# Making the down-projection's fp16 operands in the up-projection and keeping them in DRAM

## The chip, the core and the metric

The kernel runs on one core of a Trainium2 chip. The metric is the device time of one execution in microseconds; the median of several runs counts.

## What is computed

One layer of a hybrid block: four kinds of mixers on a sequence of 2048 tokens of width 1024, an output projection, and then a feed-forward part, which is where the change lies:

```python
u = rms_norm(h, norm_ffn_pre[layer])
f = jnp.square(jax.nn.relu(jnp.einsum('bsd,df->bsf', u, w_ff_up[layer])))
h = h + rms_norm(jnp.einsum('bsf,fd->bsd', f, w_ff_down[layer]), norm_ffn_post[layer])
```

Inputs and output are fp32; w_ff_up is 1024 x 4096, w_ff_down 4096 x 1024.

## The kernel before

**Products.** Every fp32 operand is split into an fp16 high and an fp16 low part (`split_to`: ACT copies to the high part, DVE subtracts for the low part), and a product is three fp16 matmuls (`mm3`). On top of that both projections multiply 2 x 2 blocks of blocks with seven products instead of eight. For that, four sums or differences of the four sub-blocks are formed first on POOL (`sums`, `diffs`), the seven operands are split in the order of `TURN`, and the results are added up behind the products. A block of the up- or down-projection is therefore seven products, numbered 0, 5, 1, 6, 4, 3, 2 in this order, into four PSUM accumulators: X (0, then 1), Y (5), Z (6, then 3) and V (4, then 2). Behind product 0 ACT copies X to s; DVE adds Y to s; behind 6 and 4 DVE makes c = s + Z and c += V; behind 3 and 2 it makes s + Z and s + V. An accumulator is written again only when it has been read.

**Up-projection** (`up_block`, called by `run`). The 4096 columns of f are 16 pairs g of 2 x 128; the tokens are two halves cp of 1024. A block (g, cp) is 84 matmuls of 128x512. `up_weights` prepares the weights of a pair up to two pairs ahead: two loads ur, two gain products (ur) and four sums (us) on POOL, a reduce for each load on DVE (a_up) and a maximum over them (m_up), which a small product p_up on PE spreads over the partitions, and seven splits (uw). `down_top` reads the rows of w_ff_down (dr) for their maximum (a_dn). Behind the products ACT applies relu and square into the tiles e, which `put` stores to DRAM (fD) as fp32, two stores a block.

**Down-projection** (`down_block`). The 16 pairs are taken in the six passes of `PASSES`: two of two pairs, four of three. A pass goes through eight blocks (cp, j) of 128 + 128 tokens, adding into the tiles y, which stay in SBUF. `down_weights` prepares the weights of a pass (dr, four differences ds on POOL, seven splits dw). For each block `f_operands` loads the fp32 f (fr), forms four sums on POOL (ft) and splits seven operands (fo) of 128 x n x 128, n being the pairs of the pass. In passes 1 to 5 POOL adds s to three of the four y parts. In the last pass `finish` normalizes: the sum of squares on ACT (fsq), ms_f, the product with the gain and rs_f on POOL, the last scaling on DVE, and the store.

**Order.** The program is recorded as operations in lanes, and `weave` writes them out by a list schedule: at each step it takes the operation with the earliest start by its own cost table, plus a tenth of a microsecond for each step of the lane's priority number. The engines then run their queues in that order, and SP issues all transfers from one queue. The up-blocks have priority number 2, the weights 1, the down-blocks 0. Nearly all instructions are recorded in one helper line, so the views name L557 for all of them.

Of the kernel before, what the change touches and what calls it, by code (L numbers as in the profile page):

```python
# [10 lines left out]
F32 = mybir.dt.float32  # L11
F16 = mybir.dt.float16
# [7 lines left out]
P = 128  # L20
# [11 lines left out]
U = 1024.0  # L32
UF = 256.0
TURN = (0, 5, 1, 6, 4, 3, 2)
PASSES = ((0, 2), (2, 4), (4, 7), (7, 10), (10, 13), (13, 16))
EPS = 1e-6
LAM_INIT = 0.8 - 0.6 * math.exp(-0.3 * 0)
# [58 lines left out]
class Halves:  # L96


    def __init__(self, tiles):
        self.tiles = tiles  # L100
        self.n = tiles[0].shape[1]
# [1477 lines left out]
def split_to(nc, src, hi, lo, scale=None):  # L1579
    if scale is None:  # L1580
        nc.scalar.activation(hi, src, AF.Copy)
        nc.vector.tensor_tensor(lo, src, hi, op=ALU.subtract)
    else:
        nc.scalar.activation(hi, src, AF.Copy, scale=scale)
        nc.vector.scalar_tensor_tensor(lo, src, scale, hi, op0=ALU.mult, op1=ALU.subtract)
# [29 lines left out]
class Ffn:  # L1615
# [8 lines left out]
    def __init__(self, k, w_up, w_dn, post, gain, u, ev, out):  # L1624
        self.k, self.w_dn, self.post, self.gain, self.u, self.ev, self.out = k, w_dn, post, gain, u, ev, out
        self.up = w_up.rearrange("(k p) f -> p k f", p=P)
        self.pairs = DFF // (2 * P)
        self.k0 = k.keep.tile([P, self.pairs], F32, tag="k0", name="k0")
        self.kd = k.keep.tile([P, self.pairs], F32, tag="kd", name="kd")
        self.f = [[k.dram.tile([4, P, 2 * (p1 - p0), 2 * P], F32, tag=f"fD{q}{cp}", name=f"fD{q}{cp}")  # L1630
                   for cp in range(2)] for q, (p0, p1) in enumerate(PASSES)]
        self.w, self.d, self.n = {}, {}, 0

    def banks(self, wide):
        self.n += 1
# [63 lines left out]
    def up_block(self, g, cp):  # L1699

        k, nc = self.k, self.k.nc
        u, w = self.u[cp], self.w[g]

        def prod(ps, i, fresh):
            for kt in range(4):
                with nc.fuse():
                    mm3(nc, ps, w[i][:, 0, kt, :], w[i][:, 1, kt, :], u[i][0][:, kt, :], u[i][1][:, kt, :], kt == 0,
                        kt == 3, fresh)

        def add(b):  # L1710
            c = self.ev.tile([P, 512], F32, tag="q", name=f"c{g}{cp}")
            nc.vector.tensor_tensor(c[:], s[:], b, op=ALU.add)
            return c

        def act(src, f, ab):
            d = e[f][:, :, ab, :]
            nc.scalar.activation(d, src.rearrange("p (j t) -> p j t", j=4), AF.Relu, scale=2.0 ** -24)
            nc.scalar.activation(d, d, AF.Square)

        def put(f):  # L1720
            x = 2 * (g - PASSES[q][0]) + f
            nc.sync.dma_start(self.f[q][cp][:, :, x, :].rearrange("j p c -> p j c"),
                              e[f][:].rearrange("p j a t -> p j (a t)"))
        q = next(i for i, (p0, p1) in enumerate(PASSES) if p0 <= g < p1)
        with nc.lane("up", 2):
            X, Y, Z, V = self.banks(False)
            nc.need(*u[TURN[-1]])
            s = k.fuw.tile([P, 512], F32, tag="s", name=f"us{g}{cp}", bufs=1)
            e = [k.fuw.tile([P, 4, 2, P], F32, tag="er", name=f"e{g}{cp}{f}", bufs=2) for f in range(2)]
            prod(X, 0, True)  # L1730
            nc.scalar.activation(s[:], X, AF.Copy)
            prod(Y, 5, True)
            nc.vector.tensor_tensor(s[:], s[:], Y, op=ALU.add)
            prod(X, 1, False)
            act(X, 0, 0)
            prod(Z, 6, True)
            c = add(Z)
            prod(V, 4, True)
            nc.vector.tensor_tensor(c[:], c[:], V, op=ALU.add)
            act(c[:], 1, 1)  # L1740
            prod(Z, 3, False)
            act(add(Z)[:], 1, 0)
            put(1)
            prod(V, 2, False)
            act(add(V)[:], 0, 1)
            put(0)

# [12 lines left out]
                split_to(nc, src, w[:, 0], w[:, 1], self.kd[:, g:g + 1])  # L1762

    def f_operands(self, q, cp, j):
        k, nc = self.k, self.k.nc
        n = PASSES[q][1] - PASSES[q][0]
        with nc.lane("fprep", 1):
            fr = k.fdr.tile([P, n, 2, 2, P], F32, tag="fr", name=f"fr{q}{cp}{j}", bufs=2)
            nc.sync.dma_start(fr[:].rearrange("p n f a t -> p (n f a t)"),
                              self.f[q][cp][j].rearrange("p f c -> p (f c)"))  # L1770
            x = fr[:, :, 0, 0, :], fr[:, :, 1, 0, :], fr[:, :, 0, 1, :], fr[:, :, 1, 1, :]
            z = [k.fue.tile([P, n, P], F32, tag="ct", name=f"ft{q}{cp}{j}", bufs=4)[:] for _ in range(4)]
            sums(nc.gpsimd, *x, *z)
            ops = {}
            for i, src in in_turn(*x, *z, False):
                w = ops[i] = k.fdr.tile([P, 2, n, P], F16, tag="fo", name=f"fo{q}{cp}{j}{i}", bufs=10)
                split_to(nc, src, w[:, 0], w[:, 1])
        return ops

    def down_block(self, q, cp, j):  # L1780

        k, nc = self.k, self.k.nc
        p0, p1 = PASSES[q]
        ops = self.f_operands(q, cp, j)
        ta, tb = cp * 8 + j, cp * 8 + 4 + j
        y, last = self.y, len(PASSES) - 1
        y11, y12, y21, y22 = y[ta][:, 0:512], y[ta][:, 512:], y[tb][:, 0:512], y[tb][:, 512:]

        def prod(ps, i, fresh):
            for x in range(p1 - p0):  # L1790
                w = self.d[p0 + x][i]
                with nc.fuse():
                    mm3(nc, ps, ops[i][:, 0, x, :], ops[i][:, 1, x, :], w[:, 0], w[:, 1], x == 0, x == p1 - p0 - 1, fresh)

        def add(o, a, b):
            nc.vector.tensor_tensor(o, a, b, op=ALU.add)
        with nc.lane("down", 0):
            if q == 0 and cp + j:
                nc.claim(y[ta], y[tb])
            X, Y, Z, V = self.banks(True)  # L1800
            s = k.fue.tile([P, 512], F32, tag="s", name=f"ds{q}{cp}{j}", bufs=2)[:]
            prod(X, 0, True)
            nc.scalar.activation(s, X, AF.Copy)
            prod(Y, 5, True)
            add(s, s, Y)
            if q:
                for o in (y22, y21, y12):
                    (nc.gpsimd if q < last or o is not y12 else nc.vector).tensor_tensor(o, o, s, op=ALU.add)
            prod(X, 1, False)
            if q:  # L1810
                add(y11, y11, X)
            else:
                nc.scalar.activation(y11, X, AF.Copy)
            prod(Z, 6, True)
            add(y22, y22 if q else s, Z)
            prod(V, 4, True)
            add(y22, y22, V)
            prod(Z, 3, False)
            add(y21, y21 if q else s, Z)
            prod(V, 2, False)  # L1820
            add(y12, y12 if q else s, V)
        if q == last:
            lo, hi, full = slice(0, 512), slice(512, D), slice(0, D)
            if (cp, j) == (1, 3):
                self.finish([(ta, lo), (tb, hi), (tb, lo), (ta, hi)])
            else:
                self.finish([(tb, full)])
                self.finish([(ta, full)])
# [32 lines left out]
    def run(self):  # L1861
        k, nc = self.k, self.k.nc
        n = self.pairs
        blocks = [(0, 0), (1, 0), (0, 1), (1, 1)] + [(g, cp) for g in range(2, n - 1) for cp in range(2)]
        blocks += [(n - 1, 1), (n - 1, 0)]
        ready = 0
        for g, cp in blocks:
            while ready < min(n, g + 2):
                self.up_weights(ready, 1)
                self.down_top(ready)  # L1870
                ready += 1
            self.up_block(g, cp)
        self.down_scale()
        self.y = [k.fd.tile([P, D], F32, tag=f"y{t}", name=f"y{t}") for t in range(NT)]
        for q, (p0, p1) in enumerate(PASSES):
            for g in range(p0, p1):
                self.down_weights(g, 2 if q else 0)
            if q == len(PASSES) - 1:
                with nc.lane("prep"):
                    self.gp = k.wpool.tile([P, D], F32, tag="wraw", name="fgp", bufs=2)  # L1880
                    nc.sync.dma_start(self.gp[:], self.post.to_broadcast([P, D]))
            for cp in range(2):
                for j in range(4):
                    self.down_block(q, cp, j)
# [133 lines left out]
```

## Time and profile before

| | us |
|---|---|
| three runs | 2641.31, 2648.63, 2649.54 |
| median | 2648.63 |
| the profiled execution, its own time | 2646.39 |
| its span | 2644.6 |

| engine | busy, us | share of the span |
|---|---|---|
| PE | 2457.6 | 93% |
| DVE | 1851.6 | 70% |
| ACT | 1294.7 | 49% |
| POOL | 1239.7 | 47% |

Shares are averages over the whole kernel; the mixers end at about 1300 us, the up-projection runs to about 1980, the down-projection to the end. Times in a view are microseconds from the start of the span. A view of groups gives, for each kind of instruction, the engine, the operation, output<-inputs by the program's tile names (numbers left out), the shapes, the count, and behind the bar the busy time in us and the mean of one in ns, then the engine's idle time ahead of them with what ended it. Matmul records overlap, so their pitch is read from the starts.

### The profile page before, as it was taken

The page shows a single profiled execution, that of the slowest core. Times are in us where ns is not written, and L with a number is a line of the kernel's source. Part 1 is how long each engine was busy: PE and PEld are TensorE (multiplying, and loading weights), DVE is VectorE, ACT ScalarE, POOL GpSimd, SP SyncE. Part 2 cuts the span into 40 slices and gives each one's busy share as a digit, 9 for nine tenths or more (in the row PEclk, how much of TensorE's full clock was granted, in tenths as well). Part 3 has the DMA queues.
Part 4 walks back from the last instruction along what each step waited for, and adds up shares of the span by engine and source line. Part 5 has one row for each costly group of instructions (what it writes and reads, how often), then busy time and mean ns, then how long its engine had stood idle before and what let it go on. Part 6 is the DMA issues. An engine that isn't in the chain of part 4 may idle for free.

```text
span 2644.6 us, 39843 instructions
## 1 busy us (share of the span) xinstructions
PE 2457.6 (93%) x14186; PEld 1298.7 (49%) x14186; DVE 1851.6 (70%) x3900; ACT 1294.7 (49%) x2647; POOL 1239.7 (47%) x1195
## 2 busy tenths in 40 slices
PE   7999999999999997988897999999998889898987
PEld 5555575656645565654444444444443334343433
DVE  6487986666798778766534555444459997979787
ACT  6377775434456676644444444444445443433332
POOL 5373331020265445447444222222235787878798
PEclk9999999999999998998997999999999999999999
DMA  6522225362351525235342433333333222222145
GB/s 185 152 70 85 83 74 186 71 183 45 82 152 53 149 83 162 83 113 159 112 128 88 128 113 126 119 99 117 120 108 123 76 89 68 88 67 90 64 143 155
DMA packets 276982, 290.30 MB, mean 110 GB/s; under 512 B 50420, under 2 KB 234676, under 8 KB 276271
## 3 DMA queue, kind: packets, MB, share of 16 engines
q1 hardware_dynamic: 276783, 287.75, 35.8%
q8 instruction: 112, 1.84, 0.3%
q14 instruction: 87, 0.71, 0.1%
HBM read 203.47 MB, written 91.04 MB: 111 GB/s over the span
## 4 chain that ended last, share of the span: by engine, by line
PE 31%; POOL 12%; DVE 8%; issue 7%; DMA 2%; ACT 1%; POOLq 0%; DVEq 0%; SPq 0%; ACTq 0%
PE mz L557 7%; PE mx L557 6%; PE mv L557 6%; POOL ft L557 5%; POOL y L557 4%; PE po L557 4%; PE my L557 3%; DVE fo L557 2%; DVE dw L557 2%; DVE y L557 1%; PE fut L557 1%; POOL rs_f L557 1%; DMA dr<-in_w_ff_down_dram 1%; POOL nt L557 1%; POOL ds L557 1%
## 5 line engine op out<-in xcount | busy, mean ns | idle before, releaser
L557 PEld LDWEIGHTS <-fo 128*128 128x128 f16 x2688 | 265.7, 99 | 399.3 <-issue 92.2
L557 PEld LDWEIGHTS <-uw 128*128 128x128 f16 x2688 | 264.1, 98 | 314.7 <-issue 5.6
L557 PE MATMUL pt<-uuh,wh 128*128 128x512 f16 x640 | 244.3, 382 | 0.0
L557 PE MATMUL pt<-uuh,wl 128*128 128x512 f16 x640 | 243.7, 381 | 0.5 <-DVE wl L557 0.5
L557 PE MATMUL pt<-uul,wh 128*128 128x512 f16 x640 | 243.7, 381 | 0.0
L557 PE MATMUL mz<-dw,fo 128*128 128x512 f16 x768 | 188.9, 390 | 53.2 <-DVE y L557 53.2
L557 POOL TENSOR_TENSOR ur<-ur,g_ffn 128x1024 f32<-128x1024 f32 x32 | 61.3, 1919 | 346.9 <-DMA ur<-in_w_ff_up_dram 290.4
L557 DVE CUSTOM_DVE_ANT_0 e<-sc,strip,scf 128x512 f32<-128x512 f32 (+3 forms) x320 | 206.1, 663 | 23.5 <-PE sc L557 14.0
L557 POOL TENSOR_TENSOR y<-y,ds 128x512 f32<-128x512 f32 x112 | 167.1, 1514 | 85.3 <-DVE ds L557 85.3
L557 ACT ACTIVATE e<-e,dmn 128x1024 f32<-128x1024 f32 (+4 forms) x192 | 171.6, 896 | 47.5 <-DVE dmn L557 44.7
L557 PE MATMUL mv<-dw,fo 128*128 128x512 f16 x768 | 185.6, 385 | 4.7 <-DVE y L557 4.1
L557 PE MATMUL mx<-dw,fo 128*128 128x512 f16 x768 | 183.0, 380 | 7.2 <-ACT ds L557 3.6
L557 ACT ACTIVATE fo<-ft 128x384 f16<-128x384 f32 (+1 forms) x192 | 92.4, 484 | 193.1 <-PE mz L557 79.6
L557 PEld LDWEIGHTS <-wh 128*128 128x128 f16 x1280 | 123.2, 99 | 126.4 <-issue 22.0
L557 PE MATMUL mx<-u,uw 128*128 128x512 f16 x768 | 180.4, 385 | 0.0
L557 PE MATMUL mz<-u,uw 128*128 128x512 f16 x768 | 178.7, 379 | 0.0
L557 PE MATMUL po<-woh,mx 128*128 128x512 f16 x512 | 166.8, 394 | 12.2 <-DVE mx L557 7.1
L557 PE MATMUL mv<-u,uw 128*128 128x512 f16 x768 | 176.7, 379 | 0.0
L557 DVE TENSOR_TENSOR fo<-ft,fo 128x384 f16<-128x384 f32 (+1 forms) x192 | 146.6, 767 | 35.1 <-ACT fo L557 35.1
L557 POOL TENSOR_SCALAR e<-e,dcf 128x256 f32<-128x256 f32 (+4 forms) x96 | 76.5, 797 | 162.6 <-DVE dcf L557 129.3
L557 ACT ACTIVATE ae<-ae,mt 128x256 f32<-128x256 f32 (+1 forms) x192 | 87.3, 456 | 114.2 <-DVE mt L557 99.1
L557 POOL TENSOR_TENSOR ft<-fr 128x384 f32<-128x384 f32 (+1 forms) x96 | 117.4, 1223 | 53.9 <-PE mz L557 40.5
(324 smaller groups left out, 5620.4 us busy)
## 6 DMA issues: line engine op xcount, KB each, us to landing
dr<-in_w_ff_down_dram SPq DMA_DIRECT2D x64, 512.0 KB, 3.6
fD<-e SPq DMA_DIRECT2D x64, 512.0 KB, 3.2
fr<-fD SPq DMA_DIRECT2D x32, 768.0 KB, 4.1
ur<-in_w_ff_up_dram SPq DMA_DIRECT2D x32, 512.0 KB
wr<-in_w_in_dram SPq DMA_DIRECT2D x24, 512.0 KB
xt<-in_x_dram SPq DMA_DIRECT2D x16, 512.0 KB, 8.0
mr<-mixT SPq DMA_DIRECT2D x16, 512.0 KB, 3.8
oxr<-in_x_dram SPq DMA_DIRECT2D x16, 512.0 KB, 4.0
```

The costliest lines, as they stand in the source:

```text
L557: op.ins.append(fn(*[real(a) for a in args], **{n: real(a) for n, a in kw.items()}))
```

## The change

The down-projection's operands of passes 1 to 5 are made in the up-projection. Behind each block of pairs 2 to 15, `up_operands` (lane fform, priority number 1) forms the four sums from e on POOL (fz), splits the seven operands for all 512 tokens of a half block into fp16 (fs), and stores them in four transfers to fD, which for these passes is fp16 in the order in which the down-projection reads it. `f_operands` is then one load for these passes (fo, two buffers, all seven operands in one tile). The fp32 stores of e remain for pass 0 alone, which still makes its operands in the down-projection. `SHELF` is the order of the operands in the stored tile. The tiles e alternate between two pools, and fz and fs use buffers of the mixers' pool.

```diff
+SHELF = (0, 1, 3, 2, 4, 5, 6)
...
+        self.f = [[k.dram.tile([4, P, p1 - p0, 7, 2, P] if q else [4, P, 2 * (p1 - p0), 2 * P], F16 if q else F32,
+                               tag=f"fD{q}{cp}", name=f"fD{q}{cp}") for cp in range(2)]
+                  for q, (p0, p1) in enumerate(PASSES)]
...
-            nc.sync.dma_start(self.f[q][cp][:, :, x, :].rearrange("j p c -> p j c"),
-                              e[f][:].rearrange("p j a t -> p j (a t)"))
+            if q == 0:
+                nc.sync.dma_start(self.f[q][cp][:, :, x, :].rearrange("j p c -> p j c"),
+                                  e[f][:].rearrange("p j a t -> p j (a t)"))
...
-            e = [k.fuw.tile([P, 4, 2, P], F32, tag="er", name=f"e{g}{cp}{f}", bufs=2) for f in range(2)]
+            self.made += 1
+            er = self.fst if self.made > 4 and self.made % 2 else k.fuw
+            e = [er.tile([P, 4, 2, P], F32, tag="er", name=f"e{g}{cp}{f}", bufs=2) for f in range(2)]
...
+        if q:
+            self.up_operands(q, g - PASSES[q][0], cp, e)
+
+    def up_operands(self, q, x, cp, e):
+
+        k, nc = self.k, self.k.nc
+        with nc.lane("fform", 1):
+            a = e[0][:, :, 0, :], e[1][:, :, 0, :], e[0][:, :, 1, :], e[1][:, :, 1, :]
+            z = [self.ev.tile([P, 512], F32, tag=f"at{i % 2}", name=f"fz{q}{x}{cp}{i}")[:].rearrange("p (j t) -> p j t", j=4)
+                 for i in range(4)]
+            sums(nc.gpsimd, *a, *z)
+            src = dict(in_turn(*a, *z, False))
+            for n in range(0, 7, 2):
+                w = self.ev.tile([P, 4, 2, 2, P], F16, tag="e1", name=f"fs{q}{x}{cp}{n}")
+                m = min(2, 7 - n)
+                for i in range(m):
+                    split_to(nc, src[SHELF[n + i]], w[:, :, i, 0, :], w[:, :, i, 1, :])
+                nc.sync.dma_start(self.f[q][cp][:, :, x, n:n + m].rearrange("j p i h t -> p j (i h t)"),
+                                  w[:, :, 0:m].rearrange("p j i h t -> p j (i h t)"))
...
+            if q:
+                w = k.fdr.tile([P, n, 7, 2, P], F16, tag="fo", name=f"fo{q}{cp}{j}", bufs=2)
+                nc.sync.dma_start(w[:].rearrange("p n i h t -> p (n i h t)"),
+                                  self.f[q][cp][j].rearrange("p n i h t -> p (n i h t)"))
+                return w
...
-            ops = {}
+            w = k.fdr.tile([P, n, 7, 2, P], F16, tag="fo", name=f"fo{q}{cp}{j}", bufs=2)
             for i, src in in_turn(*x, *z, False):
-                w = ops[i] = k.fdr.tile([P, 2, n, P], F16, tag="fo", name=f"fo{q}{cp}{j}{i}", bufs=10)
-                split_to(nc, src, w[:, 0], w[:, 1])
-        return ops
+                split_to(nc, src, w[:, :, SHELF.index(i), 0, :], w[:, :, SHELF.index(i), 1, :])
+        return w
```

The schedule is written anew, and three places of it matter below. In the names, the digits behind e, c and us are the pair and the half, those behind uw, ur and a_up the pair; fz and fs carry the pass, the pair within it and the half (fs2210 belongs to pair 6, half 1).

First place, ACT and DVE around block (7, 0). On ACT, behind the block (6, 1), in the change:

```order
L558 ACTIVATE e611_18102<-c61_18113 128x4x128
L558 ACTIVATE uw8_2_18124<-us83_17943,s_up8_17941 128x512
L558 ACTIVATE e611_18102<-e611_18102 128x4x128
L558 ACTIVATE e610_18024<-c61_18122 128x4x128
L558 ACTIVATE fs2210_18096<-e611_18102 128x4x128
L558 ACTIVATE fs2212_18146<-e611_18102 128x4x128
L558 ACTIVATE e610_18024<-e610_18024 128x4x128
L558 ACTIVATE us70_18154<-mx_18085 128x512
```

Two fs copies now stand between the last relu and the last square of a block, ahead of the copy of the next block's X. On DVE in block (7, 0), before:

```order
L557 TENSOR_REDUCE a_up9_17918<-ur90_17856 128x1
L557 TENSOR_TENSOR c70_17941<-us70_17887,mz_17920 128x512
L557 TENSOR_REDUCE a_up9_17918<-ur91_17899 128x1
L557 TENSOR_REDUCE m_up9_17960<-a_up9_17918 128x1
L557 TENSOR_TENSOR c70_17941<-c70_17941,mv_17937 128x512
```

and in the change:

```order
L558 TENSOR_REDUCE a_up9_18190<-ur90_18111 128x1
L558 TENSOR_TENSOR c70_18210<-us70_18154,mz_18182 128x512
L558 TENSOR_TENSOR fs2212_18146<-fz2213_18208,fs2212_18146 128x4x128
L558 TENSOR_TENSOR fs2214_18223<-fz2210_18157,fs2214_18223 128x4x128
L558 TENSOR_TENSOR fs2214_18223<-fz2211_18188,fs2214_18223 128x4x128
L558 TENSOR_TENSOR fs2216_18231<-fz2212_18199,fs2216_18231 128x4x128
L558 TENSOR_REDUCE a_up9_18190<-ur91_18171 128x1
L558 TENSOR_TENSOR c70_18210<-c70_18210,mv_18204 128x512
L558 TENSOR_REDUCE m_up9_18265<-a_up9_18190 128x1
```

Four subtractions have come between c = s + Z and c += V, and m_up has moved behind c += V. On PE the small product p_up, which needs m_up, stood inside product 3; it now stands behind product 3 and nine matmuls of the next block's product 0, ahead of product 2 into V. In the second block of a pair three of the next block's matmuls stand there.

Second place, POOL in the same block, before:

```order
L557 TENSOR_TENSOR ur90_17856<-ur90_17856,g_ffn_513 128x8x128
L557 TENSOR_TENSOR ur91_17899<-ur91_17899,g_ffn_513 128x8x128
L557 TENSOR_TENSOR us90_17949<-ur91_17899 128x512
L557 TENSOR_TENSOR us91_17958<-us90_17949,ur90_17856 128x512
L557 TENSOR_TENSOR us92_17972<-ur90_17856,ur91_17899 128x512
L557 TENSOR_TENSOR us93_17985<-ur90_17856,us91_17958 128x512
```

and in the change:

```order
L558 TENSOR_TENSOR fz2210_18157<-e610_18024,e611_18102 128x512
L558 TENSOR_TENSOR ur90_18111<-ur90_18111,g_ffn_513 128x8x128
L558 TENSOR_TENSOR fz2211_18188<-fz2210_18157,e610_18024 128x512
L558 TENSOR_TENSOR fz2212_18199<-e610_18024 128x512
L558 TENSOR_TENSOR fz2213_18208<-e611_18102,fz2211_18188 128x512
L558 TENSOR_TENSOR ur91_18171<-ur91_18171,g_ffn_513 128x8x128
L558 TENSOR_TENSOR us90_18238<-ur91_18171 128x512
L558 TENSOR_TENSOR us91_18250<-us90_18238,ur90_18111 128x512
L558 TENSOR_TENSOR us92_18260<-ur90_18111,ur91_18171 128x512
L558 TENSOR_TENSOR us93_18280<-ur90_18111,us91_18250 128x512
```

The four sums from e stand around the first gain product and ahead of the second one. Third place, DVE at the seam between the projections (block (15, 0) is the last of the up-projection, y4 the first result tile), before:

```order
L557 TENSOR_TENSOR c150_20440<-c150_20440,mv_20433 128x512
L557 TENSOR_TENSOR c150_20478<-us150_20296,mz_20345 128x512
L557 TENSOR_TENSOR c150_20492<-us150_20296,mv_20433 128x512
L557 TENSOR_TENSOR y4_20511<-ds000_20312,mz_20391 128x512
L557 TENSOR_TENSOR y4_20511<-y4_20511,mv_20407 128x512
```

and in the change:

```order
L558 TENSOR_TENSOR c150_21118<-c150_21118,mv_21054 128x512
L558 TENSOR_TENSOR c150_21210<-us150_20957,mz_21023 128x512
L558 TENSOR_TENSOR c150_21238<-us150_20957,mv_21054 128x512
L558 TENSOR_TENSOR fs5200_21158<-e1501_21212,fs5200_21158 128x4x128
L558 TENSOR_TENSOR fs5202_21240<-e1501_21212,fs5202_21240 128x4x128
L558 TENSOR_TENSOR fs5202_21240<-fz5203_21255,fs5202_21240 128x4x128
L558 TENSOR_TENSOR fs5204_21259<-fz5200_21249,fs5204_21259 128x4x128
L558 TENSOR_TENSOR fs5204_21259<-fz5201_21251,fs5204_21259 128x4x128
L558 TENSOR_TENSOR fs5206_21264<-fz5202_21253,fs5206_21264 128x4x128
L558 TENSOR_TENSOR y4_21297<-ds000_21109,mz_21162 128x512
```

The operands of the last up-block have come between its additions and the first addition into y4. On PE the first down matmuls now stand 36 matmuls later in that block.

## Rows read from the trace of the kernel before

**Rows 1.** Windows of the up-projection (first) and of the six passes.

```profile
core 0: us, PE busy (x) PEld busy (x) DVE busy (x) ACT busy (x) POOL busy (x), PEclk, DMA share, GB/s
1500.00:1900.00 400.00, 400.00 (x1866) 183.57 (x1865) 200.46 (x341) 175.91 (x275) 96.63 (x67) 1.00 0.36 115
1953.00:2059.00 106.00, 94.53 (x412) 41.10 (x410) 97.14 (x147) 61.89 (x131) 63.78 (x58) 0.95 0.40 124
2059.00:2147.00 88.00, 75.79 (x338) 33.35 (x337) 80.82 (x116) 34.90 (x77) 71.89 (x62) 0.98 0.24 77
2147.00:2265.00 118.00, 110.88 (x504) 49.51 (x503) 97.35 (x122) 43.06 (x82) 90.75 (x68) 0.99 0.22 75
2265.00:2389.00 124.00, 114.84 (x521) 51.23 (x520) 105.21 (x131) 47.40 (x88) 95.05 (x69) 0.99 0.23 77
2389.00:2510.00 121.00, 113.31 (x508) 50.34 (x507) 101.90 (x128) 45.53 (x85) 92.15 (x67) 0.97 0.24 79
2510.00:2637.00 127.00, 108.65 (x486) 47.66 (x484) 105.19 (x115) 44.46 (x87) 117.63 (x102) 0.99 0.48 144
```

**Rows 2.** Timelines of PE, DVE and ACT in an up-block: start, us, engine, instruction.

```profile
1656.29 2.75 PE L557 MATMUL mv<-u,uw 128*128 128x512 f16 x12
1658.88 2.75 PE L557 MATMUL mx<-u,uw 128*128 128x512 f16 x12
...
1659.15 0.69 DVE L557 TENSOR_TENSOR c<-us,mv 128x512 f32<-128x512 f32 x1 [1.97 <-PE mv L557]
...
1659.87 0.63 ACT L557 ACTIVATE e<-c 128x512 f32<-128x512 f32 x1 [1.37 <-DVE c L557]
```

**Rows 3.** Groups by shape in the up-projection, 1500 to 1900 us.

```profile
L557 POOL TENSOR_TENSOR ur<-ur,g_ffn 128x1024 f32<-128x1024 f32 x22 | 41.8, 1898 | 296.7 <-DMA ur<-in_w_ff_up_dram 243.9 <-DVE kd L557 24.7 <-issue 18.0
L557 DVE SCALAR_TENSOR_TENSOR uw<-us,s_up,uw 128x512 f16<-128x512 f32 x44 | 33.0, 749 | 3.6
L557 DVE TENSOR_REDUCE a_up<-ur 128x1 f32<-128x1024 f32 x22 | 26.7, 1213 | 0.0
L557 POOL TENSOR_TENSOR us<-ur 128x512 f32<-128x512 f32 x11 | 14.0, 1275 | 0.9
```

**Rows 4.** Groups by shape in the down-projection, 1960 to 2640 us.

```profile
L557 DVE SCALAR_TENSOR_TENSOR dw<-ds,kd,dw 128x512 f16<-128x512 f32 x60 | 72.7, 1219 | 3.5 <-ACT dw L557 3.5
L557 POOL TENSOR_TENSOR ds<-dr,ds 128x512 f32<-128x512 f32 x30 | 44.2, 1473 | 18.4 <-DMA dr<-in_w_ff_down_dram 16.6 <-DVE fo L557 1.8
```

**Rows 5.** Timelines of POOL and DVE in pass 0, one collision.

```profile
2027.96 1.45 POOL L557 TENSOR_TENSOR ds<-dr,ds 128x512 f32<-128x512 f32 x1
...
2028.20 1.75 DVE L557 SCALAR_TENSOR_TENSOR dw<-ds,kd,dw 128x512 f16<-128x512 f32 x1
```

**Rows 6.** Timeline of PE behind a gap in pass 3, and the window there.

```profile
2309.98 3.11 PE L557 MATMUL mz<-dw,fo 128*128 128x512 f16 x9 [2.92 <-DVE y L557]
2312.89 2.83 PE L557 MATMUL mv<-dw,fo 128*128 128x512 f16 x9
...
2310.00:2313.00 3.00, 3.00 (x10) 1.19 (x10) 3.00 (x4) 0.00 (x0) 2.92 (x4) 0.65 0.71 262
```

**Rows 7.** Timelines of PE and POOL in a block of pass 5.

```profile
2569.18 2.11 PE L557 MATMUL mx<-dw,fo 128*128 128x512 f16 x9
...
2582.31 2.10 PE L557 MATMUL mz<-dw,fo 128*128 128x512 f16 x9 [3.17 <-DVE y L557]
...
2571.37 0.19 POOL L557 TENSOR_SCALAR ms_f<-fss 128x1 f32<-128x1 f32 x1
...
2579.43 1.34 POOL L557 TENSOR_TENSOR y<-y,ds 128x512 f32<-128x512 f32 x1
```

**Rows 8.** Timeline of PE at the first down matmuls.

```profile
1958.70 0.61 PE L557 MATMUL mx<-dw,fo 128*128 128x512 f16 x2 [2.42 <-DVE fo L557]
1960.50 1.01 PE L557 MATMUL mx<-dw,fo 128*128 128x512 f16 x2 [1.19 <-DVE dw L557]
```

**Rows 9.** Transfers by tile: KB each, median us from issue to landing.

```profile
fr<-fD SPq DMA_DIRECT2D x32, 768.0 KB, 4.1
```

More of the change, by code (lines that the diff above doesn't have):

```diff
@@ L1629, in __init__ @@
         self.kd = k.keep.tile([P, self.pairs], F32, tag="kd", name="kd")
-        self.f = [[k.dram.tile([4, P, 2 * (p1 - p0), 2 * P], F32, tag=f"fD{q}{cp}", name=f"fD{q}{cp}")
-                   for cp in range(2)] for q, (p0, p1) in enumerate(PASSES)]
-        self.w, self.d, self.n = {}, {}, 0
+        self.f = [[k.dram.tile([4, P, p1 - p0, 7, 2, P] if q else [4, P, 2 * (p1 - p0), 2 * P], F16 if q else F32,
+                               tag=f"fD{q}{cp}", name=f"fD{q}{cp}") for cp in range(2)]
+                  for q, (p0, p1) in enumerate(PASSES)]
+        self.w, self.d, self.n, self.made = {}, {}, 0, 0
     def banks(self, wide):
@@ L1792, in prod @@
                 with nc.fuse():
-                    mm3(nc, ps, ops[i][:, 0, x, :], ops[i][:, 1, x, :], w[:, 0], w[:, 1], x == 0, x == p1 - p0 - 1, fresh)
+                    mm3(nc, ps, ops[:, x, SHELF.index(i), 0, :], ops[:, x, SHELF.index(i), 1, :], w[:, 0], w[:, 1], x == 0,
+                        x == p1 - p0 - 1, fresh)
         def add(o, a, b):
@@ L1863, in run @@
         n = self.pairs
+        self.fst = k.pool("fst", side="right", on=("ub",))
         blocks = [(0, 0), (1, 0), (0, 1), (1, 1)] + [(g, cp) for g in range(2, n - 1) for cp in range(2)]
```

## The prediction

> **What bounds the kernel now.** I read three things in this order: the windows of the feed-forward part, then the groups of instructions by shape in each half of it, then the timelines of single blocks. The windows [rows 1] show two different stages. In the up-projection (1500 to 1900 us) PE is busy without a gap while DVE works half of the time and POOL a quarter. In the six passes of the down-projection DVE is busy for 82 to 92%, POOL for 60 to 93%, and PE has gaps. What the gaps cost follows from the pitch of PE: a product of 12 matmuls ends 2.59 us after the one before it [rows 2], 0.216 us a matmul. A pass over n pairs has 8 blocks of 7 x 3 x n matmuls: 72.5 us for the passes of two pairs, 108.9 us for those of three. The windows are 106 (13 of them for 60 matmuls of the last up-block), 88, 118, 124, 121 and 127 us [rows 1]: 20, 15, 9, 15, 12 and 18 us above that, some 90 in all. That is what the change can win. What it must not break is the stage without gaps.
>
> **What bounds DVE and POOL together.** A DVE subtraction with both inputs in SBUF and a POOL sum get in each other's way. In the up-projection, where they rarely meet, a scaled subtraction takes 0.75 us and a POOL sum 1.28 [rows 3]; in the down-projection they take 1.22 and 1.47 [rows 4]. One pair shows how: a POOL sum of 1.45 us runs from 2027.96, and the subtraction issued at 2028.20 lasts 1.75 us, so it got through only behind the sum [rows 5]. Additions from PSUM (0.69 [rows 2]) are not touched. So when both engines have such work in a row they alternate, at about 1.45 us a step.
>
> **What moves.** For passes 1 to 5, 40 x 4 sums, 40 x 7 copies and 40 x 7 subtractions leave the down-projection; 28 x 4, 28 x 7 and 28 x 7 of 512 columns enter the up-projection, one set behind each block from pair 2 on. On average they fit there: over a pair of blocks (36.3 us of PE) DVE gets 14 x 0.69 = 10 us on top of 18, POOL 8 x 1.28 = 10 on top of 9. The order fits less well.
>
> **The up-projection, first block of a pair.** T is the end of the last product of the block before. The addition of V starts 0.27 us after that and takes 0.69; ACT's relu and square take 0.63 each [rows 2]. In the new order (first place shown with the change) ACT does seven activations from the relu of Z to the square that finishes e, fs copies among them, and starts them late, because Z's addition stands behind DVE's own fs work: I get e ready at about T + 4.9 and the copy of X at T + 5.5. PE wants that copy at T + 4.5 (9 matmuls of X are left, then Y) and waits **1.0 us**. POOL then does an fz sum, a gain product, three fz sums and the second gain product, 4 x 1.28 + 2 x 1.90 = 8.9 us [rows 3], to T + 13.9 (second place). Only then can DVE begin the last four subtractions, and POOL begins the four us sums at the same moment: 0.69 + 3 x 1.45 = 5.0 us, to T + 18.9. Behind them on DVE stand a reduce of 1.21 [rows 3], the addition c += V of 0.69 and a small reduce of 0.15: T + 20.9. PE waits for the last one (the product that spreads the weights' maximum stands ahead of the product into V, which needs c += V too). By its own work it is there at T + 16.9, or 17.9 with the wait above: **3.0 us** idle. After a gap of 2.92 us the granted clock is 0.65 of the 2.4 GHz over 3 us, thus for most of them at 1.2 GHz, and the next 18 matmuls take 1.7 us more; after one of 3.17 us nine matmuls take their usual 2.10 [rows 6, 7]. I take 0.8. Together 4.8 us.
>
> In the second block of a pair POOL has no weights to prepare when the four subtractions come. They take 0.69 each, two weight subtractions follow, and c += V is read by about T + 14.5, where PE wants it at 14.3: nothing. The weights of pair g + 2 meet operands of pair g - 1 for g = 3 to 13, 11 times: 11 x 4.8 = **+53 us**. Bounds: 11 x 1.0 = 11 if the engines do not alternate, 11 x 5.7 = 63 if the clock falls each time. I stay near the upper one, because rows 5 show the alternation itself.
>
> The stores of f grow from 1.05 to 1.84 MB a block, 44 GB/s more on top of 115 at a DMA share of 0.36 [rows 1]. Behind them on SP stand weight loads, which by the same walk are read some 3 us or more after they land; I cost them at nothing. If that cover goes, a late load lengthens the same wait on POOL.
>
> **The down-projection.** Pass 0 still makes its operands here. New is that the last up-block's operands stand on DVE ahead of y4 += Z (third place): e at T + 3.0, four sums 5.1, a copy 0.6, four subtractions 2.8, an addition 0.7: T + 12.2, while PE has only 15 matmuls (3.2 us) to do before it needs that. 9 us of idle and some clock make +10. Against it, the down matmuls now stand behind 36 more of the last up-block, so the early waits of 2.42 and 1.19 us [rows 8] go: **+6**. In passes 1 to 4 DVE keeps six additions a block (4 us of 13.6) and the dw subtractions, POOL the y additions and ds. I leave them stalls of 3 to 5 us a pass, at the pass ends, where a dw buffer comes free only as the block runs: 88 to 76, 118 to 112, 124 to 114, 121 to 114, **-35**. The new loads of 1.38 MB have a block of 13.6 us to land in, since a second buffer holds the next block; 768 KB take 4.1 us now [rows 9].
>
> Pass 5 wins less than POOL's load there suggests. PE waits 3.17 us in each block for y += Z, which waits for a POOL chain [rows 7]: this begins at 2571.37 with ms_f, 2.2 us after the block's first matmul, runs through two gain products and ends with y += s, begun at 2579.43. The four ft sums that leave stand behind that chain. Without them ms_f still waits for the squares of the block before, and starts some 0.3 us earlier; the chain loses about a microsecond of collisions. So 2 us of the wait stay: 127 to 119, **-8**. Sum of the down-projection: +6 - 35 - 8 = **-37**, between -25 (a third of the gain of passes 1 to 4 fails) and -64 (hardly a stall stays).
>
> **The sum.** The profiled execution took 2646.4 us (span 2644.6), 2.2 below the median of the three runs. 2646.4 + 53 - 37 = 2662.
>
> **A rule of the Trainium skill.** In rows 5 DVE and POOL overlap a little: a step of 1.45 us, where 1.28 and 0.69 one after the other make 1.97. The Trainium skill (SBUF — State Buffer, section "SBUF: two separate sides") says that the port pair which the two share is an exclusive lock, held for the whole instruction. By that rule the time is that of the fourth case below; the trace bears it out only in part.
>
> **The rivals.** *Forecast, 0.42, slower:* as above, 2645 to 2680, most of it above 2656. *The operand work hides, 0.34, faster:* DVE gets its four subtractions done in a row, or the us sums come later, so that c += V is through by T + 17.9, for which 3 us are enough. For it: the average load fits, and the up-projection has no gap today. Against it: the order puts both groups behind the same gain product. The stage then costs 11, and the time is 2646 + 11 - 37 = 2620. *Balance, 0.14, no change:* the gaps are shorter and the clock holds, 11 x 3.4 = 37; 2646. *Whole instructions exclude each other, 0.05, slower:* three steps of 1.97 instead of 1.45 are 1.6 us more a pair, 11 x 1.6 = 17; 2679. *The down-projection gives less, 0.05, slower:* the clock falls at each gap (63) and only 25 come back; 2684.
>
> **How the numbers follow.** A measurement of this kernel can tell 0.3% (8 us) from no change. The forecast and the last two are slower by more, 0.52; balance 0.14; hidden 0.34. The point is the forecast's 2662. The range goes from 2612 (hidden, with 45 won below) to 2690; the forecast's own is 2645 to 2680.
>
> **What would show it.** In the profile after: a PE gap of about 3 us in each pair of up-blocks, put down to DVE, and pairs of 40 to 42 us instead of 36.3; fs subtractions at a mean near 1 us; a gap of some 9 us at the seam; passes 1 to 4 at 76, 112, 114 and 114 us; pass 5 still with waits of 2 us. If PE has no gap between 1500 and 1900 us, the forecast is wrong and the second case right.

## The result, and the profile after

| | before | after |
|---|---|---|
| median of the runs, us | 2646.61 | 2671.61 |
| lowest to highest | 2641.31 to 2649.54 | 2667.83 to 2676.44 |
| profiled execution | 2646.39 | 2676.44 |
| its span | 2644.6 | 2674.7 |

The ratio is 1.0098, with a 95% interval of 1.0072 to 1.0123: slower by 25 us. The forecast was 2662, in a range of 2612 to 2690, with slower as the likeliest outcome. The profiled execution of the change is the slowest of its four runs, 4.8 us above their median.

The profile of the change: busy time by engine, the group of the new subtractions over the whole kernel, and the new load. DVE and POOL have less to do in all, PE is busy for longer because part of the time its clock is low.

```profile
PE 2479.1 (93%) x14186; PEld 1303.5 (49%) x14186; DVE 1817.3 (68%) x3816; ACT 1256.4 (47%) x2563; POOL 1182.2 (44%) x1147
...
L558 DVE TENSOR_TENSOR fs<-fz,fs 128x512 f16<-128x512 f32 x112 | 120.6, 1136 | 27.4 <-ACT fs L558 27.3
...
fo<-fD SPq DMA_DIRECT2D x32, 1344.0 KB, 6.1
```

The windows of the change that answer to [rows 1]: the up-projection, the start of pass 0, and passes 1 to 5.

```profile
1500.00:1900.00 400.00, 369.31 (x1614) 163.64 (x1613) 309.56 (x421) 209.06 (x365) 202.00 (x135) 0.94 0.43 137
2034.00:2080.00 46.00, 27.56 (x99) 10.82 (x98) 38.11 (x51) 27.48 (x55) 26.37 (x24) 0.74 0.48 161
2150.60:2225.80 75.20, 73.73 (x341) 33.16 (x340) 45.33 (x64) 14.55 (x23) 42.38 (x32) 1.00 0.37 132
2225.80:2335.50 109.70, 108.98 (x506) 49.36 (x505) 48.50 (x66) 14.60 (x23) 42.28 (x33) 1.00 0.34 120
...
2445.10:2553.90 108.80, 108.80 (x506) 49.32 (x505) 50.20 (x69) 18.37 (x28) 45.93 (x35) 1.00 0.37 131
2553.90:2674.00 120.10, 110.21 (x505) 49.18 (x503) 69.82 (x77) 24.65 (x44) 80.19 (x83) 0.97 0.66 212
```

The two stages have changed places. The up-projection, gapless before, has PE idle for 31 of 400 us, at a mean granted clock of 0.94; passes 1 to 4 are all but gapless, with DVE busy for 44 to 60% where it was 82 to 92%.

Where the 30.1 us between the two spans lie, by fixed points of PE's own sequence (the small product p_up of a pair, the first product into Y of a pass):

| stretch | before | after | difference | forecast |
|---|---|---|---|---|
| start to p_up of pair 4 (the mixers) | 1476.3 | 1481.8 | +5.6 | 0 |
| to p_up of pair 15 (3.9 us of place taken out, 2.9 of clock behind it put in) | 396.8 | 463.6 | +65.9 | +53 |
| to pass 1 (the same 3.9 and 2.9) | 186.9 | 207.2 | +21.2 | +6 |
| passes 1 to 4 | 447.9 | 403.3 | -44.6 | -35 |
| pass 5 to the end | 136.8 | 118.8 | -18.0 | -8 |

In the change p_up of a pair stands 18 matmuls later among the same matmuls, hence the 3.9 us; the 2.9 us are what the matmuls behind the last p_up lose to a low clock (5.7 us where it is 2.8). By these points passes 1 to 4 took 88, 118, 121 and 121 us before and take 75, 110, 110 and 109 now; two of the windows in [rows 1] began a little late in their pass, which moves microseconds between passes 3, 4 and 5 and leaves the sum. The first 5.6 us lie ahead of the first p_up of all, in the mixers, which the change does not touch; over the ten profiles of this case that point lies anywhere from 1153.7 to 1164.8 us. This may be why this execution lies 4.8 us above its median, but it is not shown.

The loss, seen at one pair: DVE, POOL and PE around p_up of pair 7 (start, us, engine, instruction, and in brackets the idle time ahead of it).

```profile
1596.20 0.69 DVE L558 TENSOR_TENSOR c<-us,mz 128x512 f32<-128x512 f32 x1 [0.26 <-PE mz L558]
1597.95 6.76 DVE L558 TENSOR_TENSOR fs<-fz,fs 128x512 f16<-128x512 f32 x4 [1.06 <-ACT fs L558]
1604.63 1.21 DVE L558 TENSOR_REDUCE a_up<-ur 128x1 f32<-128x1024 f32 x1
1605.76 0.67 DVE L558 TENSOR_TENSOR c<-c,mv 128x512 f32<-128x512 f32 x1
1606.36 0.14 DVE L558 TENSOR_REDUCE m_up<-a_up 128x1 f32<-128x2 f32 x1
```

```profile
1597.22 1.89 POOL L558 TENSOR_TENSOR ur<-ur,g_ffn 128x1024 f32<-128x1024 f32 x1
1599.19 1.60 POOL L558 TENSOR_TENSOR us<-ur 128x512 f32<-128x512 f32 x1
1600.87 1.63 POOL L558 TENSOR_TENSOR us<-us,ur 128x512 f32<-128x512 f32 x1
1602.45 1.72 POOL L558 TENSOR_TENSOR us<-ur,ur 128x512 f32<-128x512 f32 x1
1604.12 1.71 POOL L558 TENSOR_TENSOR us<-ur,us 128x512 f32<-128x512 f32 x1
```

```profile
1601.18 2.11 PE L558 MATMUL mx<-u,uw 128*128 128x512 f16 x9
1606.56 0.80 PE L558 MATMUL p_up<-ident,m_up 128*128 128x128 f32 x2 [3.27 <-DVE m_up L558]
1607.14 4.09 PE L558 MATMUL mv<-u,uw 128*128 128x512 f16 x12
1611.07 0.81 PE L558 MATMUL mx<-u,uw 128*128 128x512 f16 x3
```

Four subtractions take 6.76 us: the first gets through behind the gain product, the rest alternate with the four us sums, at 1.64 us a step (from 1599.19 to 1604.12). Then the reduce, c += V and m_up; PE, done with its nine matmuls, has waited 3.27 us. Behind the gap the twelve matmuls into V, which take 2.59 us from start to start without a gap, take 3.93. The window of that stretch and of the one a pair later:

```profile
1606.50:1611.00 4.50, 4.45 (x14) 2.08 (x15) 2.03 (x8) 3.94 (x7) 0.00 (x0) 0.63 0.02 6
1648.30:1654.00 5.70, 5.68 (x14) 2.34 (x15) 1.99 (x7) 3.90 (x7) 0.00 (x0) 0.50 0.02 5
```

The granted clock is 0.63 and 0.50 of the 2.4 GHz: in the second stretch 1.2 GHz throughout. There are ten such gaps, at the p_up of pairs 6 to 15, of 3.23 to 3.82 us; the weights of pair 5, the eleventh case, show as a gap of 3.97 us one product earlier. From p_up of pair 6 to that of pair 15 a pair takes 42.3 us on the mean, where it took 36.5.

### The profile page after: what moved, and what is told of

It reads as the page before. It is cut to its first block, busy times and chain, and to the rows that moved or that the text cites. A ratio compares the mean times of both kernels' runs of the same rounds, so it can differ in the third digit from the quotient of the medians.

```text
span 2674.7 us, 39514 instructions
## 1 busy us (share of the span) xinstructions
PE 2479.1 (93%) x14186; PEld 1303.5 (49%) x14186; DVE 1817.3 (68%) x3816; ACT 1256.4 (47%) x2563; POOL 1182.2 (44%) x1147
## 4 chain that ended last, share of the span: by engine, by line
PE 29%; DVE 11%; POOL 9%; issue 5%; ACT 4%; DMA 2%; DVEq 0%; POOLq 0%; SPq 0%; ACTq 0%
PE mv L558 7%; PE mx L558 6%; PE mz L558 5%; PE po L558 4%; POOL fz L558 4%; DVE fs L558 3%; PE my L558 3%; POOL y L558 2%; ACT e L558 1%; DVE fo L558 1%; DVE dw L558 1%; DVE y L558 1%; DMA ur<-in_w_ff_up_dram 1%; ACT fs L558 1%; DVE uw L558 1%
## 5 line engine op out<-in xcount | busy, mean ns | idle before, releaser
L558 PEld LDWEIGHTS <-uw 128*128 128x128 f16 x2688 | 269.6, 100 | 341.7 <-issue 45.3
L558 POOL TENSOR_TENSOR y<-y,ds 128x512 f32<-128x512 f32 x112 | 145.7, 1326 | 217.8 <-DVE ds L558 217.8
L558 DVE CUSTOM_DVE_ANT_0 e<-sc,strip,scf 128x512 f32<-128x512 f32 (+3 forms) x320 | 205.8, 662 | 24.4 <-PE sc L558 15.8
L558 PE MATMUL mv<-u,uw 128*128 128x512 f16 x768 | 196.2, 409 | 0.6 <-DVE c L558 0.6
L558 PE MATMUL mz<-dw,fo 128*128 128x512 f16 x768 | 183.5, 382 | 8.9 <-DVE y L558 8.8
L558 POOL TENSOR_TENSOR fz<-e,e 128x512 f32<-128x512 f32 x28 | 36.8, 1313 | 280.1 <-ACT e L558 280.1
L558 DVE TENSOR_TENSOR fs<-fz,fs 128x512 f16<-128x512 f32 x112 | 120.6, 1136 | 27.4 <-ACT fs L558 27.3
L558 ACT ACTIVATE ds<-mx 128x512 f32<-128x512 f32 x48 | 28.5, 593 | 231.9 <-PE mx L558 231.9
L558 PEld LDWEIGHTS <-mx 128*128 128x128 f16 x768 | 76.9, 102 | 105.2 <-issue 13.3
```

The lines of the kernel that those rows point to most:

```text
L558: op.ins.append(fn(*[real(a) for a in args], **{n: real(a) for n, a in kw.items()}))
```

## Experiments

The theory: the up-projection loses because of *where* the new work stands. DVE's last four fs subtractions meet POOL's us sums, and c += V and m_up queue behind them. Its rival: the *amount* of new work is too much for DVE, ACT or the store queue, wherever it stands.

**No us sums, same order** (no_us). The sums of the weights shrink to a column from pair 5 on, while the schedule is written with their old cost (lines left out are marked).

```diff
-            sums(nc.gpsimd, *q, *z)
+            if 5 <= g:
...
+                sums(nc.gpsimd, *[t[:, :, 0:1] for t in q], *[t[:, :, 0:1] for t in z])
...
+                z = [t[:, :, 0:1].to_broadcast([P, 4, P]) for t in z]
+            else:
+                sums(nc.gpsimd, *q, *z)
```

> Leaves out: the four sums us of the up-projection's weights from pair 5 on write one column in 128, and their splits read that column over and over; every engine's order is that of the change. Theory (DVE's subtractions and POOL's sums alternate): behind the second gain product the four fs subtractions go on at 0.65 us each, c += V and m_up are through before PE has done its nine matmuls, the gaps of 3.2 us ahead of p_up go from pair 5's on, the clock stays at its upper level, pairs of up-blocks fall from 42.3 to 36.5-37 us, and the time from 2672 to 2612-2622. Rival (the sheer amount of new work on DVE, ACT and SP, wherever it meets): gaps of 2 us or more stay, pairs of 40 us or more, 2650 or above.

Measured in one run: 2616.19 us, beside 2648.99 for the kernel before on the same chip. The up-projection's window; the group of subtractions in it, in the change and then in this run; and PE at the p_up of pair 10, the only gap above 0.04 us ahead of a p_up from pair 5 on:

```profile
1500.00:1900.00 400.00, 396.81 (x1830) 179.06 (x1828) 318.61 (x483) 236.61 (x416) 184.48 (x154) 1.00 0.48 153
```

```profile
L558 DVE TENSOR_TENSOR fs<-fz,fs 128x512 f16<-128x512 f32 x75 | 89.5, 1252 | 15.3 <-ACT fs L558 15.3
...
L561 DVE TENSOR_TENSOR fs<-fz,fs 128x512 f16<-128x512 f32 x84 | 66.0, 845 | 17.3 <-ACT fs L561 17.3
```

```profile
1703.06 0.49 PE L561 MATMUL p_up<-ident,m_up 128*128 128x128 f32 x2 [0.61 <-DVE m_up L561]
```

The fs<-fz subtractions fall from a mean of 1252 ns to 845, the gaps go, the clock is 1.00, a pair takes 37.0 us. DVE and ACT still carry all of the operands' work, so their amount is not it. The run took away POOL work and its collision together; which of the two counts, the next one tells.

**One priority number** (late6).

```diff
-        with nc.lane("fform", 1):
+        with nc.lane("fform", 6):
```

> The whole change with one number other: the lane of the stored operands has priority number 6 in place of 1, which puts a_up, m_up and c += V ahead of the fs subtractions and the us sums ahead of the fz sums. Theory (the place of the work decides, not its amount): no PE gap over 0.5 us in the up-projection, pairs of 36.5-37.5 us, the seam and the passes as in the change: 2605-2622. Rival (amount): the collisions only move, to the splits uw or to s += Y, and PE waits there: pairs of 39-41 us, 2640-2660.

Measured: 2606.09 us, ratio to before 0.9835 (0.9820 to 0.9851). The window, the group of subtractions that now collides, DVE ahead of the p_up of pair 10, and the longest gap left, at the seam:

```profile
1500.00:1900.00 400.00, 400.00 (x1865) 183.56 (x1864) 347.74 (x494) 252.42 (x428) 225.89 (x154) 1.00 0.49 158
```

```profile
L558 DVE TENSOR_TENSOR fs<-e,fs 128x512 f16<-128x512 f32 x66 | 79.1, 1236 | 0.0
```

```profile
1697.36 0.15 DVE L558 TENSOR_REDUCE m_up<-a_up 128x1 f32<-128x2 f32 x1
1697.51 0.69 DVE L558 TENSOR_TENSOR c<-c,mv 128x512 f32<-128x512 f32 x1
```

```profile
2009.05 1.44 PE L558 MATMUL mx<-dw,fo 128*128 128x512 f16 x3 [14.81 <-ACT ds L558]
```

All the work of the change is there, DVE is busy for 87% of the stage, and PE has no gap: a pair takes 36.48 us, as in the kernel before. The collisions have not gone (the subtractions straight from e now have a mean of 1236 ns, 686 in the change), but nothing that PE wants stands behind them. The whole 66 us of the up-projection were a matter of the order. The same number has also moved p_up back to its old place on PE; but in no_us, with p_up where the change has it, the gaps went too, so that place alone is not the cause. The seam costs what it costs in the change: 206.4 us from p_up of pair 15 to pass 1, 19.5 above the kernel before, whose p_up has the same place.

**Pair 1 last** (seam). Block (15, 0) with its stored operands no longer ends the up-projection.

```diff
-        blocks = [(0, 0), (1, 0), (0, 1), (1, 1)] + [(g, cp) for g in range(2, n - 1) for cp in range(2)]
-        blocks += [(n - 1, 1), (n - 1, 0)]
+        pairs = [0] + list(range(2, n)) + [1]
+        blocks = [(0, 0), (2, 0), (0, 1), (2, 1)] + [(g, cp) for g in range(3, n) for cp in range(2)]
+        blocks += [(1, 0), (1, 1)]
...
-            while ready < min(n, g + 2):
-                self.up_weights(ready, 1)
-                self.down_top(ready)
+            while ready < min(n, pairs.index(g) + 2):
+                self.up_weights(pairs[ready], 1)
+                self.down_top(pairs[ready])
```

> The change with the up-blocks in another order: pair 1, whose operands are made in pass 0, comes last instead of pair 15, so no stored operands are made beside the start of pass 0. Theory (the seam's 18 us of gaps are the last two blocks' operands on ACT and DVE ahead of pass 0's own): the gaps of 6.9, 3.5 and 7.9 us go, from the last p_up to pass 1 takes some 18 us less; one more pair meets weights of another in the up-projection, 6 us: 2656-2664. Rival (the first gaps are a late load of the fp32 operands, the queue being full of stores): 10 us of gaps stay, 2664-2674.

Measured: 2662.73 us, ratio 1.0043 (1.0030 to 1.0057). From the last p_up to pass 1 it is 191.6 us instead of 207.2, 15.5 less. The medians show 9 of it, or 11 when each is set against its own runs of the kernel before. The up-projection gives some back: it has gaps of 3.1, 3.5 and 3.8 us at its start that the change does not all have, and from the fourth p_up to the last it takes 489.6 us, 3.2 more for the same matmuls. The gap of 7.9 us is gone. The first two are not. PE, and then POOL's first ft sum:

```profile
2044.25 1.03 PE L558 MATMUL mx<-dw,fo 128*128 128x512 f16 x2 [4.11 <-ACT fo L558]
...
2048.39 1.04 PE L558 MATMUL mx<-dw,fo 128*128 128x512 f16 x2 [3.11 <-DVE fo L558]
```

```profile
2040.22 0.73 POOL L558 TENSOR_TENSOR ft<-fr 128x256 f32<-128x256 f32 x1 [29.08 <-PE mv L558]
```

So the theory is right for the last gap, and for the first two only in part: 7.2 of 10.4 us stay when no stored operand is near. The rival's late load is not seen here: the trace puts the wait of POOL's first ft sum down to PE's last products into V and not to a transfer. That reads as a wait for buffers which the last up-block still holds; a run below tests it. In the change itself that first sum, at 2033.76, did wait 2.46 us for the load of the fp32 operands; but DVE, whose subtraction PE waited for, worked from 2032.09 on without a pause.

**Both edits** (both6).

> Priority number 6 and pair 1 last, together. Theory: both gains add up, the up-projection at PE's pitch, no gap over 3 us at the seam: 2585-2602, thus 1.7 to 2.4 % below the kernel before. Rival (late6's collisions move): 2625-2645.

Measured: 2600.04 us, ratio 0.9824 (0.9796 to 0.9853). The two do not add up: 2606 by one, and the other brings 6 us more instead of 9 to 16, and these 6 us are not clear of the spread (2596.80 to 2612.05 here, 2602.13 to 2610.53 there). The traces tell more: from the last p_up to pass 1 it is 193.8 us, 12.7 less than with the number alone, but from the fourth p_up to the last it is 427.6, 8.0 more, with gaps of 0.3 to 1.5 us around the sixth to the eighth. Two gaps at the first down matmuls are left:

```profile
1980.68 0.60 PE L558 MATMUL mx<-dw,fo 128*128 128x512 f16 x2 [4.11 <-ACT fo L558]
1984.81 1.03 PE L558 MATMUL mx<-dw,fo 128*128 128x512 f16 x2 [3.52 <-DVE fo L558]
```

**Freeing the buffers earlier** (best6). The buffers of pass 0's first operands lie where half 1 of u was, so half 1 of pair 1 goes first, and pass 0 begins with half 1. Against the kernel with both edits:

```diff
-        blocks += [(1, 0), (1, 1)]
+        blocks += [(1, 1), (1, 0)]
...
-            if q == 0 and cp + j:
+            if q == 0 and (cp, j) != (1, 0):
...
-            for cp in range(2):
+            for cp in (range(2) if q else (1, 0)):
```

> Priority number 6; pair 1 last, its half 1 ahead of its half 0, and pass 0 takes half 1 first, so that the buffers of the first operands of pass 0 come free one block earlier and its work has PE's last up-block beside it, as in the kernel before. Theory (the 7 us that pass 0 still waits at its start in the run with both edits are a matter of these buffers): the gaps of 4.1 and 3.5 us at the first down matmuls shrink to some 3 in all, 2590-2597. Rival (pass 0's own sums and splits take that time anywhere): 2598-2604.

Measured: 2599.52 us, ratio 0.9821 (0.9809 to 0.9834), the same as without, and in the rival's range. The buffers did hold up the first operands: the gaps of 4.1 and 3.5 us at the first down matmuls are gone. But freeing them wins nothing: from the last p_up to pass 1 it is 192.5 us, 1.3 less, since the last up-block pays instead, its copy of X standing on ACT behind pass 0's splits:

```profile
1968.67 5.23 PE L558 MATMUL mx<-u,uw 128*128 128x512 f16 x12 [4.87 <-ACT us L558]
```

**A larger number** (best12), the same kernel with 12 in place of 6.

> The same with priority number 12. Theory (place, not amount): as with 6, within 4 us of it, no gap over 0.5 us per pair in the up-projection. Rival (the stored operands now hold up the blocks' tiles e or the splits): gaps of 1-3 us a pair, 2605-2630.

Measured: 2634.41 us, ratio 0.9952 (0.9935 to 0.9970), outside both ranges. From the ninth p_up on a pair takes 41.8 us on the mean again, with gaps of 1.7 to 2.9 us at p_up. POOL, DVE and PE around one of them:

```profile
1695.26 1.90 POOL L558 TENSOR_TENSOR ur<-ur,g_ffn 128x1024 f32<-128x1024 f32 x1 [2.18 <-DMA ur<-in_w_ff_up_dram]
1697.23 1.60 POOL L558 TENSOR_TENSOR us<-ur 128x512 f32<-128x512 f32 x1
```

```profile
1695.53 5.52 DVE L558 TENSOR_TENSOR fs<-fz,fs 128x512 f16<-128x512 f32 x3
1700.97 1.21 DVE L558 TENSOR_REDUCE a_up<-ur 128x1 f32<-128x1024 f32 x1
```

```profile
1702.89 0.80 PE L558 MATMUL p_up<-ident,m_up 128*128 128x128 f32 x2 [2.83 <-DVE m_up L558]
```

The order has put three fs subtractions ahead of the second a_up once more, against the us sums. It looks like the change's own loss by another route; but here POOL also waits for the weights' load, 2.18 us ahead of the gain product, and no run separates the two. A later lane is not in itself a better one.

**What pass 5 gains, by halves** (p5_nosum, p5_nosub). Both are the kernel before with one half of pass 5's operand work shrunk to a column, the orders unchanged: POOL's four ft sums, or DVE's seven fo subtractions.

```diff
-            sums(nc.gpsimd, *x, *z)
+            if q < 5:
+                sums(nc.gpsimd, *x, *z)
+            else:
...
+                sums(nc.gpsimd, *[a[:, :, 0:1] for a in x], *[a[:, :, 0:1] for a in z])
...
+                z = [a[:, :, 0:1].to_broadcast([P, n, P]) for a in z]
```

> The kernel before; leaves out, in pass 5 alone, the four ft sums of each block (one column in 128 is done and read over and over); orders unchanged. Theory A: ms_f still begins 1.5 us or more behind the block's first matmul, blocks of 16 us or more, as the prediction said of the waits, the time falls by 4-10 us. Theory B: blocks of 14-14.5 us as in the change, the time falls by 14-20 us.

```diff
-                split_to(nc, src, w[:, 0], w[:, 1])
+                if q < 5:
+                    split_to(nc, src, w[:, 0], w[:, 1])
+                else:
+                    nc.scalar.activation(w[:, 0], src, AF.Copy)
...
+                    nc.vector.tensor_tensor(w[:, 1, :, 0:1], src[:, :, 0:1], w[:, 0, :, 0:1], op=ALU.subtract)
...
```

> The kernel before; leaves out, in pass 5 alone, the seven subtractions of each block's operands (one column in 128 is done, and the high part stands in for the low one); orders unchanged. Theory A (DVE's subtractions hold up the additions into y, so the squares, ms_f and POOL's chain come late): ms_f begins less than 1 us behind a block's first matmul instead of 2.2, blocks of 17.3 us fall to 15.5 or less, the time by 10-14 us. Theory B (POOL's own load makes the chain long): blocks stay at 16.5 or more, the time falls by 0-6 us.

Measured: 2639.86 us without the sums (ratio 0.9970, 0.9951 to 0.9988) and 2636.81 without the subtractions (0.9961, 0.9946 to 0.9975), beside 2647.35: 7.5 and 10.5 us less. From pass 5's first product into Y to the end of the span it is 129.3 and 125.0 us, where it was 136.8. PE's first matmul of a block, ms_f on POOL and PE's wait in that block, first without the sums, then without the subtractions:

```profile
2545.94 2.11 PE L559 MATMUL mx<-dw,fo 128*128 128x512 f16 x9
...
2546.91 0.19 POOL L559 TENSOR_SCALAR ms_f<-fss 128x1 f32<-128x1 f32 x1 [1.97 <-ACT fsq L559]
...
2557.56 2.10 PE L559 MATMUL mz<-dw,fo 128*128 128x512 f16 x9 [1.74 <-DVE y L559]
```

```profile
2551.09 2.11 PE L559 MATMUL mx<-dw,fo 128*128 128x512 f16 x9
...
2552.45 0.19 POOL L559 TENSOR_SCALAR ms_f<-fss 128x1 f32<-128x1 f32 x1
...
2562.00 2.10 PE L559 MATMUL mz<-dw,fo 128*128 128x512 f16 x9 [1.03 <-DVE y L559]
```

Neither chain alone made the block long. Without the sums POOL waits 1.97 us for the squares, which wait for DVE's additions; without the subtractions the squares are early, and ms_f follows straight on POOL's own sums, which end at 2552.37. Blocks of 17.3 us become 15.8 and 15.2, with both gone, in the change, 13.9. By the traces the two halves win 7.5 and 11.8 us of pass 5, and the change 18.0.

## Why the prediction was right, and what it mis-sized

The direction, the range and the mechanism held; the forecast was 10 us low because two errors nearly cancelled: 28 us too little lost up to pass 1, 20 us too little won behind it. That the sum came so near is luck; the place and the length of the wait in the up-projection are not.

- **The collision behind the second gain product** was right in place and size. Forecast: the gain product done at T + 13.9, m_up at T + 20.9, a wait of 3.0 us. At pair 8, T is 1627.90: the product ended at T + 13.0, PE resumed at T + 20.4, after 3.23 us. no_us and late6 show the cause twice, by the sums and by the order.
- **The clock behind the gap**, taken at 0.8 us a pair, is the term that failed. From p_up to the next block's matmuls the ten gaps give 5.0 us on the mean, 4.4 to 5.7, where it is 2.8 without a gap: 2.2 us each. [Rows 7] had a gap of 3.17 us without a loss, and I took the middle; here no gap of that length went free, and the upper bound of 1.7 was too low too. Over ten pairs that is 14 us, about what the up-projection lost beyond the forecast (13). The trace of the kernel before had a warning that I did not read: of its five gaps of 3.16 to 3.17 us in pass 5 the last one was followed by a granted clock of 0.66, and the 18 matmuls behind it took 5.57 us, where those behind the other four took 4.15.

```profile
2616.83 2.77 PE L557 MATMUL mz<-dw,fo 128*128 128x512 f16 x9 [3.16 <-DVE y L557]
...
2616.80:2621.00 4.20, 4.17 (x13) 1.63 (x13) 3.34 (x4) 0.51 (x1) 0.51 (x1) 0.66 0.79 214
```

- **The wait for ACT's copy of X**, 1.0 us, was 0.2 in the block where it was expected: ACT had it ready at T + 4.7, not 5.5.
- **The step of the alternation** took 1.64 us, more than the 1.45 of [rows 5] and less than the 1.97 of a sum and a subtraction one after the other. The Trainium skill (SBUF — State Buffer, section "SBUF: two separate sides") has the shared port pair held for a whole instruction; the trace agrees with it in part, somewhat more than the prediction's single pair showed.
- **The seam**, +6, came to about +21. The 9 us behind the last up-block's operands were right in size (7.9), but PE waits there for ACT's copy of X, which stands behind the fs copies, and not for DVE's addition. "The early waits of 2.42 and 1.19 us go" was wrong: the first down matmuls wait 6.88 us, and then the up-block's own product into Z waits 3.50 for an addition on DVE. Standing behind 36 more matmuls of the up-block did not help, in part because the fs work of block (15, 1) stands on ACT and DVE between pass 0's own operands: four copies from 2035.94, and four subtractions of 3.6 us in all before the first fo subtraction at 2042.76. The timeline of ACT with the copies of both blocks, and that of PE:

```profile
2035.94 2.17 ACT L558 ACTIVATE fs<-fz 128x512 f16<-128x512 f32 x4
...
2071.39 2.19 ACT L558 ACTIVATE fs<-fz 128x512 f16<-128x512 f32 x4 [5.15 <-POOL fz L558]
```

```profile
2044.30 1.89 PE L558 MATMUL mx<-dw,fo 128*128 128x512 f16 x4 [6.88 <-DVE fo L558]
...
2074.60 1.44 PE L558 MATMUL mx<-dw,fo 128*128 128x512 f16 x3 [7.89 <-ACT ds L558]
```

  Only a part of the early waits comes from this: with pair 1 last 7.2 us of them remained, and with the buffers freed earlier they moved to the last up-block. How the rest of the 10.4 us divides in the change itself stays open.
- **Passes 1 to 4**: forecast 76, 112, 114 and 114, measured 75, 110, 110 and 109. The stalls that I left at the pass ends are hardly there: 403 us, where PE's own pitch makes 399.
- **Pass 5**, -8: I took away POOL's sums and kept 2 us of wait "since ms_f still waits for the squares of the block before". p5_nosum measures just that: 7.5 us, waits of 1.74. What I left out is that the squares themselves wait for y += V on DVE, and DVE loses seven subtractions a block. In the change ms_f starts 0.1 us after the block's first matmul (at 2595.66), where it started 2.2 after it [rows 7], and PE's wait for y += Z is gone:

```profile
2595.80 0.19 POOL L558 TENSOR_SCALAR ms_f<-fss 128x1 f32<-128x1 f32 x1 [3.81 <-ACT fsq L558]
...
2603.24 1.35 POOL L558 TENSOR_TENSOR y<-y,ds 128x512 f32<-128x512 f32 x1
```

- **The stores**, costed at nothing, cost nothing: late6 moves 158 GB/s through the stage without a gap. In best12 POOL does wait for the weights' load.

The second case of the prediction, the hidden operand work, is what late6 measures: c += V and m_up ahead of the four subtractions, and nothing lost in the up-projection. It came to 2606 where 2620 was worked out: the 11 us for the wait on ACT's copy did not come, and from the last p_up on the trace gives 43 us where 37 were forecast.

## What to carry to other kernels

When work moves into a stage with room on average, read what stands in the queues behind it: 10 us of sums and 10 us of subtractions a pair cost nothing or 66 us in all, by whether the one addition that PE waits for is in front of them or behind. Cost a short gap of PE by what the clock does after it as well as by its length. When a chain has two inputs (here POOL's sums, and squares that wait for DVE), removing the load of one exposes the other: price both before leaving a wait in the sum. Here one priority number of one lane turned 2672 us into 2606, 1.7% below the kernel before; the block order on top of it (2600) brought no more than the spread of the runs.

## What the runs showed of the hardware that I had not expected

All ten gaps of 3.2 to 3.8 us ahead of p_up, each after some 39 us of matmuls, were followed by a granted clock of 0.50 to 0.65 over 4.4 to 5.7 us, and cost 1.6 to 2.9 us on top. The length of a gap alone does not tell: of the five gaps of 3.16 to 3.17 us that recur every 17 us in pass 5 before, four cost nothing and one 1.4 us, and in best12 a gap of 2.56 us ahead of p_up cost 1.7 us where one of 2.67 cost nothing.

A sum of 3 or 4 columns on POOL took 0.20 us wherever DVE was idle, added from PSUM or reduced a single tile. Beside a DVE instruction with two inputs in SBUF it lasted 0.05 to 0.07 us longer than that one still ran: 0.38 to 1.18 us in p5_nosum, 0.52 to 0.65 in no_us, where the sums of 512 columns take 1.27 in the kernel before.
